# A decoder layer on one core: the sample group's value steps stand one tile later in the cross-attention's output projection

## The chip, the cores and the metric

The kernel runs on one core of a Trainium2 chip. The metric is the device time of one execution in microseconds (us): the median of the timed runs. A profile is one execution of the same program, recorded by the hardware profiler.

## What is computed

One layer of a hybrid decoder for 512 prompt tokens and 64 sample tokens (8 samples of 8 tokens), which share all weights: a mixing block (Mamba-2 heads and mLSTM heads), then cross-attention to a memory, then a SwiGLU block, each with a norm ahead of it and another behind it. The change lies in the cross-attention:

```python
u = _rms(x) * g_pre_x
qx = (u @ w_xq).reshape(bsz, length, X_HEADS, X_HEAD_DIM)
sc = jnp.einsum('blhd,bmhd->bhlm', qx, mem_k) * (X_HEAD_DIM ** -0.5)
pr = jax.nn.softmax(sc, axis=-1)
o = jnp.einsum('bhlm,bmhd->blhd', pr, mem_v).reshape(bsz, length, X_WIDTH) @ w_xo
x = x + _rms(o) * g_post_x
```

There are 4 heads of 256 and 256 memory entries. The prompt's keys and values are computed from its memory; each of the 8 samples has its own cached keys and values, read from HBM. All is in float32.

## The kernel before

Activations lie feature by token: 8 blocks of 128 features, 576 tokens, of which 0 to 511 are the prompt's and 512 to 575 the samples'. A float32 product is made of three matmuls in a faster format: each operand is split into a high part (a copy by ScalarE, ACT, L180 for weights) and a low part (the rest, by VectorE, DVE, L187), and high x high (L202), high x low (L203) and low weight x high (L205) are added up in PSUM (`gemm`, L195).

**The output projection** (L1492 to L1531) has 8 tiles of 128 output features, j = 0 to 7, counted from 0 here. Its first pass takes the tokens 0 to 287 (`EHALVES[0]`); a second pass over the tokens 288 to 575 follows from a written-out plan. A tile has 8 blocks of 3 matmuls with 288 columns. `xo(j, 0)` takes a PSUM bank and asks `split_w` (L172) for the tile's weights: a 512 KB load on SyncE's queue (SP) into one of two buffers `raw`, a cast to `whi` on ACT, a subtraction to `wlo` on DVE. A `raw` buffer is free when the tile two before is split. The split weights of tiles 0 to 3 and 7 come from one pool of three, those of 4, 5 and 6 from another; so tile 3 takes the place of tile 0. The blocks go in the order 2 to 7, then 0 and 1, because the blocks 0 and 1 are head 0's output, which is written last (`attn_values`, the matmuls `ps_ov` of L1372 to L1374, ACT's and DVE's split L191 and L192). Tiles 0 to 2 are given as six blocks and then, in order behind each other, two blocks. Tile 3 does its low-weight products late. After a tile ACT squares it (L264, L268) and scales it (L1504), and DVE adds the squares (L269).

**The samples' attention** is a chain of generators that are advanced a half at a time. `attn_samples_v(hb)` (L1426) does the values for four samples. `pick` (L1389) loads a sample's cached values in two parts of 512 KB (`cached`, L1383, on SP's queue) into a ring of buffers; three are called kva, one kvb. For each part four narrow matmuls (L1399, one a head, weights 128 x 32, 256 columns) go into a bank `ps_os`. Two samples, so 4 loads and 16 matmuls, make a half; the profile counts two records for each of these matmuls, 32 a half. DVE then picks the wanted rows (L1405, L1407). After the second half PE transposes the result (L1432), ACT copies it to the high part of the attention output's sample columns (L1436) and DVE writes the low part (L1437). These columns are read by the second pass only. The last generator, `attn_samples_v(0)`, is not advanced inside the loop over heads; its two halves are left for the projection.

**What sets the order.** The kernel is written with a tile framework whose scheduler orders the instructions of each engine by a timeline model. `with tc.issue_after(m.ins)` holds what is written in the block behind instruction m; `sample_step(m)` (L1270) advances the generator inside such a block. `ends[j]` is the last matmul of tile j. The loads that a step issues belong to it, so they move with it in SP's queue; each waits until the matmuls that read the ring's buffer before are done.

Of the kernel before, what the change touches and what calls it, by code (L numbers as in the profile page):

```python
# [115 lines left out]
def build(nc, tc, ctx, I, O):  # L116
# [593 lines left out]
    for g in range(2):  # L710
# [13 lines left out]
        for h in range(8):  # L724
            k, j = h % 2, (8 * g + h) // 2
# [542 lines left out]
    steps = iter(())  # L1268

    def sample_step(m):  # L1270

        with tc.issue_after(m.ins):
            next(steps, None)
# [137 lines left out]
    def attn_samples_k(hb):  # L1411
        pr, pt = s5[:, 3072 + 256 * hb:3328 + 256 * hb], s5[:, 3584 + 256 * hb:3840 + 256 * hb]
        yield from pick(pr, hb, I["kc"], lambda h, d: qsm[:, 2 * h + d, 32 * hb:32 * hb + 32], "ps_sa")
        mx = at.tile([P, 1], F32, name="mxs")
        sm = at.tile([P, 1], F32, name="sms")
        V.reduce_max(mx, pr, axis=AX.X)
        V.tensor_scalar(mx, mx, -1.0 / 16.0, None, op0=ALU.mult)
        A.activation(pr, pr, AF.Exp, scale=1.0 / 16.0, bias=mx, accum_out=sm)
        V.reciprocal(sm, sm)
        V.tensor_scalar(pr, pr, sm, None, op0=ALU.mult)  # L1420
        pst = (B0, B1)[hb]("ps_pts")
        for m in range(2):
            TE.transpose(pst[:, m * P:(m + 1) * P], pr[:, m * P:(m + 1) * P], ident)
        A.copy(pt, pst[:, 0:256])

    def attn_samples_v(hb):  # L1426
        pt, ot = s5[:, 3584 + 256 * hb:3840 + 256 * hb], s5[:, 4096 + 256 * hb:4352 + 256 * hb]
        tt = slice(TP + 32 * hb, TP + 32 * hb + 32)
        yield from pick(ot, hb, I["vc"], lambda h, m: pt[:, m * P + 32 * h:m * P + 32 * h + 32], "ps_os")
        pst = (B0, B1)[hb]("ps_ots")  # L1430
        for dv in range(2):
            TE.transpose(pst[:, dv * P:(dv + 1) * P], ot[:, dv * P:(dv + 1) * P], ident)  # L1432
        p4 = pst[:, 0:256].rearrange("p (d h t) -> p h d t", d=2, h=4)
        oh4 = oh[:, :, tt].rearrange("p (h d) t -> p h d t", d=2)
        ol4 = ol[:, :, tt].rearrange("p (h d) t -> p h d t", d=2)
        A.copy(oh4, p4)  # L1436
        V.tensor_tensor(ol4, p4, oh4.bitcast(F32), op=ALU.subtract)  # L1437
# [29 lines left out]
    for h in range(3, -1, -1):  # L1467
# [11 lines left out]
        steps = attn_samples_k(h - 2) if h > 1 else attn_samples_v(h)  # L1479
# [12 lines left out]
    def xo(j, i, pool=None):  # L1492

        t0, n = EHALVES[i]

        with tc.issue_after(evx[j - 3].ins if j > 2 else ovs[5].ins):
            ps, w = GP("ps_xo")[:, :n], weights(("xo", j), I["wxo"][j], pool=pool, cut=1024)

        def step(k0, k1):
            m = gemm(ps, [(*w, KT)], act(oh), act(ol), t0, n, k0, k1, [2, 3, 4, 5, 6, 7, 0, 1], 6 if j == 3 else 0)  # L1500
            if k1 < KT:
                return m
            add_sq(ph, ssq, ps, j if i == 0 else XO1.index(j), n, t0=t0)
            evx.append(A.activation(f[:, j, t0:t0 + n], ps, AF.Copy, scale=PAR("g_postx", j)))  # L1504
            return m, evx[-1]
        return step
# [10 lines left out]
    for j in range(8):  # L1517
        step = xo(j, 0, wx if 3 < j < 7 else None)
        if j < 3:

            step(0, KT - 2)
            with tc.issue_after(ends[-1].ins) if j else ExitStack():
                ends.append(step(KT - 2, KT)[0])
        else:
            ends.append(step(0, KT)[0])

        if j == 1:
            next(steps, None)
        elif j == 4:
            sample_step(ends[-1])  # L1530
    kxs.close()  # L1531
    u3l = SL(5, "u3l", F32R)
# [821 lines left out]
```

## Time and profile before

| | us |
|---|---|
| runs | 1088.58, 1088.96, 1090.29 |
| median | 1088.96 |
| profiled execution | 1087.01 |
| its span, first to last instruction | 1085.2 |
| TensorE busy in it | 1075.0 |

The output projection's first pass runs from about 624 us to 660 us of the span. In the profile, PE is TensorE, PEld its weight loads, DVE VectorE, ACT ScalarE, POOL GpSimd, and SPq the issuing of DMAs by SyncE. A row of the timeline gives the start, the us until the last of its instructions ended, the engine, the source line, the operation, output and inputs by the program's names, the shape and the count; in square brackets stands the idle time of that engine ahead of it and what ended it. Matmuls are pipelined, so rows overlap. A row on DMAs gives what was loaded, the queue, the count, the size, and the median us from issue to landing.

### The profile page before, as it was taken

To read this page: it belongs to the slowest core of one execution; us is meant where nothing else is said; L and a number is where in the kernel's file an instruction comes from. 1 tells how busy PE (TensorE), PEld (TensorE's weight loads), DVE (VectorE), ACT (ScalarE), POOL (GpSimd) and SP (SyncE) were. 2 spreads that over 40 slices of the span, in tenths; PEclk is the share of its full clock that TensorE was granted. 3 is DMA by queue.
4 is the path that set the end of the run, shared out by engine and by line. 5 is a ranking of instruction groups with operands and counts; after the bars stand their busy time and mean duration, and the time that the engine had idled before them with its cause. 6 is when DMAs were issued, how large, how long until landed. Compare 5 with 4: busy or idle time off the path is not lost.

```text
span 1085.2 us, 20708 instructions
## 1 busy us (share of the span) xinstructions
PE 1075.0 (99%) x8124; PEld 1022.1 (94%) x8124; DVE 752.4 (69%) x1507; ACT 610.9 (56%) x1098; POOL 228.0 (21%) x305
## 2 busy tenths in 40 slices
PE   9999999999999999999999999999999999999997
PEld 9999887778999999999999989999999999999997
DVE  6896785658877775568755546766467887787556
ACT  7867632355654555656555545645566566656653
POOL 1332643313113111000154301100011111111000
PEclk9999999999999999999999999999999999999999
DMA  6775535435654449653458775643486697578532
GB/s 211 179 159 126 161 111 172 165 80 185 190 152 144 110 123 324 226 193 101 152 194 288 271 252 180 239 133 92 135 176 137 159 203 163 117 189 184 125 131 88
DMA packets 58966, 182.29 MB, mean 168 GB/s; under 512 B 6604, under 2 KB 11852, under 8 KB 58356
## 3 DMA queue, kind: packets, MB, share of 16 engines
q1 hardware_dynamic: 42740, 138.06, 38.6%
q0 software_dynamic: 15552, 41.95, 19.6%
q8 instruction: 64, 1.05, 0.4%
q10 hardware_dynamic: 576, 0.95, 0.3%
q14 instruction: 34, 0.28, 0.1%
HBM read 160.28 MB, written 20.65 MB: 167 GB/s over the span
## 4 chain that ended last, share of the span: by engine, by line
PE 86%; DVE 5%; ACT 4%; issue 2%; DMA 2%; POOL 0%; DVEq 0%; SPq 0%; ACTq 0%; POOLq 0%
PE ps_in L203 4%; PE ps_in L202 4%; PE ps_in L205 4%; PE ps_v L815 3%; PE ps_o L205 3%; PE ps_o L203 3%; PE ps_g L1846 3%; PE ps_g L1847 3%; PE ps_o L202 3%; PE ps_u L1847 3%; PE ps_u L1848 3%; PE ps_u L1846 3%; PE ps_g L1848 3%; PE ps_dn L1846 2%; PE ps_dn L1847 2%
## 5 line engine op out<-in xcount | busy, mean ns | idle before, releaser
L202 PE MATMUL ps_in<-uh,whi 128*128 128x320 f32 (+1 forms) x544 | 162.9, 300 | 0.5 <-DVE cb L451 0.5
L205 PE MATMUL ps_in<-uh,wlo 128*128 128x320 f32 (+1 forms) x544 | 162.3, 299 | 0.3 <-DMA wlo<-win 0.3
L203 PE MATMUL ps_in<-ul,whi 128*128 128x320 f32 (+1 forms) x544 | 161.8, 298 | 0.0
L180 ACT CAST whi<-raw 128x1024 fp32r<-128x1024 f32 (+1 forms) x104 | 105.2, 1013 | 100.0 <-PE ps_in L203 25.9
L187 DVE TENSOR_TENSOR wlo<-raw,whi 128x512 fp32r<-128x512 f32 (+1 forms) x96 | 93.7, 978 | 75.1 <-ACT whi L180 74.0
L202 PEld LDWEIGHTS ps_in<-uh,whi 128*128 128x128 f32 x544 | 102.8, 189 | 3.3 <-issue 1.7
L205 PEld LDWEIGHTS ps_in<-uh,wlo 128*128 128x128 f32 x544 | 102.3, 188 | 1.5 <-DMA wlo<-win 0.5
L203 PEld LDWEIGHTS ps_in<-ul,whi 128*128 128x128 f32 x544 | 102.4, 188 | 0.6
L185 POOL DMA_DIRECT2D wlo<-win x32 | 27.8, 869 | 80.7 <-ACT wlo L184 70.0
L1847 PE MATMUL ps_g<-b,whi 128*128 128x288 f32 x144 | 42.5, 295 | 0.0
L1846 PE MATMUL ps_g<-b,whi 128*128 128x288 f32 x144 | 42.4, 295 | 0.0
L1847 PE MATMUL ps_u<-b,whi 128*128 128x288 f32 x144 | 42.4, 295 | 0.0
L1846 PE MATMUL ps_u<-b,whi 128*128 128x288 f32 x144 | 42.2, 294 | 0.0
L1819 ACT CAST whi<-rawx 128x1024 fp32r<-128x1024 f32 (+1 forms) x26 | 25.6, 984 | 27.9 <-PE ps_dn L1847 13.8
L192 DVE TENSOR_TENSOR wlo<-sw,whi 128x1024 fp32r<-128x1024 f32 (+1 forms) x26 | 29.6, 1140 | 14.9 <-ACT whi L191 14.8
L202 PE MATMUL ps_xo<-qh,whi 128*128 128x288 f32 x128 | 38.5, 303 | 0.2 <-ACT whi L180 0.2
L205 PE MATMUL ps_o<-mixm_h,wlo 128*128 128x256 f32 (+1 forms) x128 | 37.9, 296 | 0.0
L1798 ACT CAST whi<-raw 128x1024 fp32r<-128x1024 f32 (+1 forms) x26 | 25.6, 983 | 21.8 <-PE ps_g L1847 9.7
L203 PE MATMUL ps_xo<-ql,whi 128*128 128x288 f32 x128 | 37.8, 296 | 0.0
L205 PE MATMUL ps_o<-mixs_h,wlo 128*128 128x320 f32 (+1 forms) x128 | 37.7, 295 | 0.0
L203 PE MATMUL ps_o<-mixs_l,whi 128*128 128x320 f32 (+1 forms) x128 | 37.7, 295 | 0.0
L203 PE MATMUL ps_o<-mixm_l,whi 128*128 128x256 f32 (+1 forms) x128 | 37.7, 295 | 0.0
(769 smaller groups left out, 3853.6 us busy)
## 6 DMA issues: line engine op xcount, KB each, us to landing
raw<-win SPq DMA_DIRECT2D x35, 512.0 KB, 4.0
raw<-wout SPq DMA_DIRECT2D x17, 512.0 KB, 3.7
raw<-wxq SPq DMA_DIRECT2D x13, 512.0 KB, 6.0
raw<-wgate SPq DMA_DIRECT2D x13, 512.0 KB, 3.6
raw<-wup SPq DMA_DIRECT2D x13, 512.0 KB, 5.1
wlo<-win POOLq DMA_DIRECT2D x24, 256.0 KB, 5.1
kva<-vc SPq DMA_DIRECT2D x11, 512.0 KB, 5.0
raw<-wv SPq DMA_DIRECT2D x10, 512.0 KB, 4.0
```

The lines of the kernel that those rows point to most:

```text
L180: casts.append(A.copy(hi[:, :n], raw[:, :n]))
L185: G.dma_start(lo[:, a:b], src[:, a:b], accum_op=ALU.add)
L187: e.tensor_tensor(lo[:, a:b], raw[:, a:b], hi[:, a:b].bitcast(F32), op=ALU.subtract)
L192: (eng or V).tensor_tensor(lo, src, hi.bitcast(F32), op=ALU.subtract)
L202: mm(ps, wh, ah, start=i == 0, stop=False)
L203: mm(ps, wh, al, start=False, stop=False)
L205: m = mm(ps, tiles[order[c]][1], xh(order[c], t0, n), start=False, stop=c == len(tiles) - 1)
L815: mm(ps, a, b, skip_group_check=True, **kw)
L1798: s.c1 = A.copy(s.h1[:, s.all], s.r1[:, s.all])
L1846: mm(ps, wh, b[0][k], start=start and k == 0, stop=False, skip_group_check=True)
L1847: mm(ps, wh, b[1][k], start=False, stop=False, skip_group_check=True)
L1848: m = mm(ps, wl, b[0][k], start=False, stop=k == nk - 1, skip_group_check=True)
```

## The change

Before, the first half of the last generator was advanced after tile 1 was written, without `issue_after`, so that the scheduler could place it anywhere that its data allowed; the second half was advanced behind tile 4's last matmul. Now both are advanced by `sample_step`, behind the last matmul of tile 2 and of tile 5. Counted from 0, that is ahead of tiles 3 and 6 in place of 2 and 5.

```diff
         else:
             ends.append(step(0, KT)[0])
 
-        if j == 1:
-            next(steps, None)
-        elif j == 4:
+        if j in (2, 5):
             sample_step(ends[-1])
     kxs.close()
```

The kernel after has two lines fewer from there on, so a line of the profile above L1527 is lower by two in its profile.

## The prediction

> **What bounds the kernel now.** I read the page first: busy time by engine and the chain that ended last.
>
> ```profile
> PE 1075.0 (99%) x8124; PEld 1022.1 (94%) x8124; DVE 752.4 (69%) x1507; ACT 610.9 (56%) x1098; POOL 228.0 (21%) x305
> PE 86%; DVE 5%; ACT 4%; issue 2%; DMA 2%; POOL 0%; DVEq 0%; SPq 0%; ACTq 0%; POOLq 0%
> ```
>
> TensorE (PE) is busy for 1075.0 of 1085.2 us and is 86% of the chain, so what the change adds to or takes from PE's path inside the output projection is found again at the end. No matmul is added or dropped. What can move the time is the price of the order: switches between matmul shapes, and waits. So next I read PE's timeline of the stage, 624 to 664 us. Its columns are start, time until the last of the row ended, engine, line, names, shape and count; what a matmul costs is the distance to the next start, since they overlap.
>
> ```profile
> 629.92 0.30 PE L205 MATMUL ps_xo<-qh,wlo 128*128 128x288 f32 x1
> 630.14 0.64 PE L1399 MATMUL ps_os<-kva 128*32 128x256 f32 x8
> 630.71 0.40 PE L202 MATMUL ps_xo<-qh,whi 128*128 128x288 f32 x1
> 630.95 0.30 PE L203 MATMUL ps_xo<-ql,whi 128*128 128x288 f32 x1
> 631.09 0.29 PE L205 MATMUL ps_xo<-qh,wlo 128*128 128x288 f32 x1
> 631.31 0.62 PE L1399 MATMUL ps_os<-kva 128*32 128x256 f32 x2
> 631.86 0.50 PE L1372 MATMUL ps_ov<-prh,mv 128*128 128x512 f32 x1
> 632.29 0.63 PE L1399 MATMUL ps_os<-kva 128*32 128x256 f32 x6
> 632.86 0.40 PE L202 MATMUL ps_xo<-qh,whi 128*128 128x288 f32 x1
> 633.10 0.30 PE L203 MATMUL ps_xo<-ql,whi 128*128 128x288 f32 x1
> ...
> 635.44 0.39 PE L1373 MATMUL ps_ov<-prl,mv 128*128 128x512 f32 x1
> 635.66 0.39 PE L1374 MATMUL ps_ov<-prh,mv 128*128 128x512 f32 x1
> 635.98 0.64 PE L1399 MATMUL ps_os<-kva 128*32 128x256 f32 x8
> ...
> 636.98 0.40 PE L202 MATMUL ps_xo<-qh,whi 128*128 128x288 f32 x1
> 637.22 0.29 PE L203 MATMUL ps_xo<-ql,whi 128*128 128x288 f32 x1
> ...
> 639.33 0.29 PE L205 MATMUL ps_xo<-qh,wlo 128*128 128x288 f32 x1
> ...
> 640.93 0.29 PE L205 MATMUL ps_xo<-qh,wlo 128*128 128x288 f32 x1
> 641.45 0.40 PE L202 MATMUL ps_xo<-qh,whi 128*128 128x288 f32 x1 [0.22 <-ACT whi L180]
> 641.69 0.30 PE L203 MATMUL ps_xo<-ql,whi 128*128 128x288 f32 x1
> ...
> 647.78 0.29 PE L205 MATMUL ps_xo<-qh,wlo 128*128 128x288 f32 x1
> 648.00 1.50 PE L1399 MATMUL ps_os<-kva 128*32 128x256 f32 x24
> ...
> 649.87 0.40 PE L202 MATMUL ps_xo<-qh,whi 128*128 128x288 f32 x1
> 650.11 0.29 PE L203 MATMUL ps_xo<-ql,whi 128*128 128x288 f32 x1
> ...
> 653.15 0.29 PE L202 MATMUL ps_xo<-qh,whi 128*128 128x288 f32 x1
> ```
>
> The reader is to see: the samples' narrow matmuls (128*32; 32 records a batch, 24 from kva and 8 from kvb) stand in one piece at 648.00 but in pieces between 630.14 and 636.98, and one hole of 0.22 us stands before tile 3 at 641.45. Tiles are counted from 0 throughout, as the loop does: 629.92 ends tile 1's first part, 641.45 opens tile 3, 649.87 tile 5, 653.15 tile 6. A projection matmul costs (653.15 - 650.11) / 23 = 0.132 us, a 512-wide one 635.66 - 635.44 = 0.22 to 0.23.
>
> **The change, part by part.** The scheduler decides, so I compared the order in which the two built programs issue. In the changed one the first batch stands in one piece after tile 2's last matmul, in front of tile 3; the second stands in front of tile 6. All before tile 2 is the same, and all behind the first tile of the second token half, but for a few waits.
>
> 1. *First batch in one piece.* A whole batch lengthens the path from 647.78 to 650.11 by 2.33 - 2 x 0.132 = 2.07. In pieces it costs 630.95 - 629.92 - 0.26 = 0.77; from 631.09 to 633.10 it costs 2.01 less one wide and two projection matmuls (0.49), so 1.52; from 635.66 to 637.22 it costs 1.56 - 0.23 - 0.13 = 1.20. That is 3.49, so one piece saves 1.42 us.
>
> 2. *The hole before tile 3.* From 640.93 to 641.69 go 0.76 us where two matmuls need 0.26. The batch now stands there, and its switch is paid in point 1: another 0.50 saved, if tile 3's weights are cast in time (checked in point 3).
>
> 3. *A new wait in tile 0's tail.* The last six matmuls of tiles 0 and 1 need the last attention head's output, which ACT and DVE write after PE's last ps_ov matmul. Before, that chain lay beside a batch and most of tile 2.
>
> ```profile
> 636.09 0.59 ACT L191 CAST qh<-ps_ov 128x512 fp32r<-128x512 f32 x1 [0.78 <-PE ps_ov L1374]
> 636.71 0.69 DVE L192 TENSOR_TENSOR ql<-ps_ov,qh 128x512 fp32r<-128x512 f32 x1 [0.67 <-ACT qh L191]
> 641.43 1.22 DVE L187 TENSOR_TENSOR wlo<-raw,whi 128x1024 fp32r<-128x1024 f32 x1 [3.12 <-ACT whi L180]
> ```
>
> The low part is ready at 636.71 + 0.69 = 637.40, that is 1.74 after the last ps_ov start (635.66). In the new order the last ps_ov starts at 630.05 + 16 x 0.132 + 11 x 0.23 = 634.69, two matmuls of tile 2 follow, and the fifth of the tail would start at 635.71 but needs the low part of 636.43. With the refill after a wait (the 0.24 instead of 0.13 at 641.45) and 0.05 of response, about 0.88 us is lost. Tile 0 then ends at 636.72, tiles 1 and 2 take 12 x 0.132, the batch starts at 638.52 and tile 3 at 640.39. Before, tile 0's last matmul started at 639.33; tile 3, which waited for the cast behind it, could start 2.12 later (641.45), and its split ended 3.32 later (641.43 + 1.22 = 642.65). Now that is 638.84, in time, and 640.04.
> Parts 1 to 3: -1.42 - 0.50 + 0.88 = -1.04; by the walk 640.39 - 641.45 = -1.06. I take -1.06.
>
> 4. *Tile 5's weights lose their cover.* Here SP's queue matters. SP waits in order. Before, tile 5's load stood behind all four second-half value loads; it now stands behind three (kvb's moves behind it), but each of these waits for a piece of the first batch, and these pieces come later.
>
> ```profile
> 608.84 0.33 SPq L175 DMA_DIRECT2D raw<-wxo  x1
> 609.26 1.08 SPq L1386 DMA_DIRECT2D kva<-vc  x2
> 610.46 0.36 SPq L1386 DMA_DIRECT2D kvb<-vc  x1
> ...
> 636.68 0.33 SPq L1386 DMA_DIRECT2D kva<-vc  x1
> 637.11 1.35 SPq L1386 DMA_DIRECT2D kvb<-vc  x1
> 642.68 0.33 SPq L175 DMA_DIRECT2D raw<-wxo  x1
> ```
>
> ```profile
> kvb<-vc SPq DMA_DIRECT2D x1, 512.0 KB, 6.9
> ```
>
> ```profile
> kva<-vc SPq DMA_DIRECT2D x1, 512.0 KB, 7.2
> ```
>
> ```profile
> kvb<-vc SPq DMA_DIRECT2D x3, 512.0 KB, 6.1
> ```
>
> ```profile
> 646.14 1.05 ACT L180 CAST whi<-raw 128x1024 fp32r<-128x1024 f32 x1 [0.41 <-DMA raw<-wxo]
> 647.28 1.23 DVE L187 TENSOR_TENSOR wlo<-raw,whi 128x1024 fp32r<-128x1024 f32 x1 [1.45 <-ACT whi L180]
> ```
>
> The last number of a kva or kvb row is us from issue to landing. The first of these rows is the load issued at 610.46, the second is the third load of another burst, the third the middle of the stage's three kvb loads. Before, tile 5's load went out at 642.68 with the value loads nearly all landed, landed near 646.1 (3.4 later), was cast and split by 648.51, and first needed at 649.87: the second batch lay in between. Now the third piece of the batch ends at 638.52 + 1.50 = 640.02, its load goes out at 640.08 (SP follows by 0.06), and tile 5's load 0.43 behind it, 640.5; tile 3's split (640.04), which frees its buffer, is no later. Three fresh loads of 512 KB are ahead of it. Tile 5 now follows tile 4 directly: first matmul at 640.39 + 0.11 + 48 x 0.132 = 646.84, the third, which needs the low part, at 647.10. Landing to split takes 2.43, or 2.45 with PE's response. So there is no wait for a landing up to 644.65, 4.15 after issue; beyond that PE loses landing + 2.45 - 647.10, and 0.11 of refill. Bounds for the landing: 3.4 (a lone load) and 7.2. The likest rows are fourth-in-burst loads, 6.9 (behind the three at 608.84 and 609.26) and 6.1; I take 6.5, so 647.0, and a loss of 2.35 + 0.11 = 2.46 us.
>
> The DMA page of the Trainium skill, "DMA: Bandwidth & Descriptors", in "Queues, rings and completion order", says that each DMA engine takes descriptors in ring order; by that the load waits for the three ahead, which the 6.9 against 3.4 bears out. [...]
>
> 5. *What I cost at nothing.* GpSimd's queue is unchanged. DVE's two reads of the first batch move behind tile 3's and 4's splits; only the transposes some 15 us later wait for them. kvb's load moves behind tile 5's: its reader, the second batch, is 10 us off. Tile 6's cast moves behind tile 4's evacuation and tile 7's ahead of tile 5's; tile 6 starts a batch and 24 matmuls after tile 5, so each has over 2 us. The last transposes (L1432) go from tile 6 to the sixth matmul of tile 7, with 18 x 0.132 = 2.4 us of matmuls behind them instead of over 5, and their ACT copy now stands behind a 1.05 us cast. That cast starts when tile 6 is evacuated, about a microsecond before the transposes, so about half a microsecond is to spare; without it the second token half would wait, microsecond for microsecond.
>
> **Sum:** -1.06 + 2.46 = +1.4 us. The profiled execution took 1087.01 us (span 1085.2), 1.95 below the median of the runs shown, 1088.96; on the median that is 1090.4.
>
> **Rivals.**
> - *The load lands as if alone.* 3.4 us after issue, 643.9, no wait at tile 5; parts 1 to 3 stay: -1.06, so 1087.9. For it: the load at 642.68 did that. Against: three value loads go out within 1.3 us ahead of it.
> - *Slower, by sharing.* If the loads in flight share the engines' time, tile 5's lands with the last of five (kvb behind it too). Four loads took from 608.84 to 610.46 + 6.9 = 617.36, so 8.5 us; beyond a lone 3.4 that is 1.7 each. From the first issue, 638.52 + 0.64 + 0.06 = 639.2, five land by 639.2 + 3.4 + 4 x 1.7 = 649.4, PE loses 4.86, net +3.8, so 1092.8. It ends slower by over 0.2% from a landing 7.3 after issue. For it: the 7.2 of a third-in-burst load. Against: the 6.1.
> - *The change does nothing*: the scheduler could have put the batches back. The issue order rules that out.
>
> **How the numbers follow.** 0.2% is about what a measurement of this kernel can tell from no change: 2.2 us here. My forecast, a wait of 1.5 to 3.3 us at tile 5 with a net between +0.4 and +2.2, gets 0.60; the lone landing, and landings up to +0.4, 0.19, of which 0.03 for over 2.2 us gained by something unseen; sharing, or a wait that I cost at nothing, 0.21. So faster 0.03, within 0.76, slower 0.21. The range runs from the first rival less half a microsecond, 1087.4, to the 7.2 us landing (+2.1) and some way into the sharing case, 1091.8.
>
> **What would show it.** Right: one batch before tile 3 with no hole; a wait on ACT or DVE for ql in tile 0's tail; tile 3 about 1 us earlier; then tile 5 waiting 2 to 3 us for whi or wlo, and the cast in front waiting for raw<-wxo; tile 6 about 1.4 us later than 653.15. Wrong: tile 5 without a wait (the landing was misjudged), tile 3 not earlier (parts 1 to 3), or a wait at the second token half (part 5).

## The result and the profile after

| | us |
|---|---|
| before, beside the changed kernel | 1088.77 (1087.69 to 1090.29) |
| after | 1093.10 (1092.04 to 1093.38) |
| ratio | 1.0038, 95% interval 1.0025 to 1.0051 |
| profiled execution of after, its span | 1092.55, 1090.8 |

So the change costs 4.3 us; 1.4 were forecast, and the time lies outside the range. The page of the changed kernel looks as the old one did:

```profile
PE 1078.0 (99%) x8124; PEld 1025.2 (94%) x8124; DVE 753.5 (69%) x1507; ACT 611.5 (56%) x1098; POOL 227.4 (21%) x305
```

As many matmuls as before, 3.0 us more of busy TensorE, in a span 5.6 us longer. An unchanged count with more busy time means that some matmuls became dearer, which the page alone can't place. PE's timeline of the stage, with the columns as before, does:

```profile
630.41 0.30 PE L205 MATMUL ps_xo<-qh,wlo 128*128 128x288 f32 x1
...
636.46 0.29 PE L202 MATMUL ps_xo<-qh,whi 128*128 128x288 f32 x1
636.99 0.40 PE L203 MATMUL ps_xo<-ql,whi 128*128 128x288 f32 x1 [0.23 <-DVE ql L192]
637.22 0.29 PE L205 MATMUL ps_xo<-qh,wlo 128*128 128x288 f32 x1
...
638.81 0.29 PE L205 MATMUL ps_xo<-qh,wlo 128*128 128x288 f32 x1
639.04 1.50 PE L1399 MATMUL ps_os<-kva 128*32 128x256 f32 x24
...
640.90 0.40 PE L202 MATMUL ps_xo<-qh,whi 128*128 128x288 f32 x1
...
647.22 0.29 PE L205 MATMUL ps_xo<-qh,wlo 128*128 128x288 f32 x1
649.68 0.40 PE L202 MATMUL ps_xo<-qh,whi 128*128 128x288 f32 x1 [2.16 <-ACT whi L180]
649.91 0.29 PE L203 MATMUL ps_xo<-ql,whi 128*128 128x288 f32 x1
650.99 0.61 PE L205 MATMUL ps_xo<-qh,wlo 128*128 128x288 f32 x1 [0.79 <-DVE wlo L187]
651.40 0.44 PE L202 MATMUL ps_xo<-qh,whi 128*128 128x288 f32 x1
651.64 0.44 PE L203 MATMUL ps_xo<-ql,whi 128*128 128x288 f32 x1
...
656.20 0.44 PE L205 MATMUL ps_xo<-qh,wlo 128*128 128x288 f32 x1
656.57 1.68 PE L1399 MATMUL ps_os<-kva 128*32 128x256 f32 x24
...
658.61 0.40 PE L202 MATMUL ps_xo<-qh,whi 128*128 128x288 f32 x1
```

The row at 630.41 was at 629.92 before: this execution reaches the stage 0.49 us later, and that much is taken off below. The reader is to see four things. The first batch now stands in one piece before tile 3 (639.04). Tile 3 follows it at 640.90 without a hole. Tile 5 waits twice, 2.16 us for its cast and 0.79 for its low part. And from 651.40 to 656.20 the matmuls start 0.24 us apart, not 0.132, and a record lasts 0.44, not 0.29, although nothing waits any more. Tile 6 comes at 658.61 - 0.49 = 658.12, against 653.15 before: 4.97 later.

The load behind that wait, in the issues of SP's queue, in the two loads of the stage's weights by themselves (the last number is us from issue to landing; the first row is tile 5's, the second tile 6's), and in the cast that waited for it:

```profile
639.74 1.28 SPq L1386 DMA_DIRECT2D kva<-vc  x3
641.11 0.56 SPq L175 DMA_DIRECT2D raw<-wxo  x1
```

```profile
raw<-wxo SPq DMA_DIRECT2D x1, 512.0 KB, 7.4
```

```profile
raw<-wxo SPq DMA_DIRECT2D x1, 512.0 KB, 8.8
```

```profile
648.58 1.04 ACT L180 CAST whi<-raw 128x1024 fp32r<-128x1024 f32 x1 [3.40 <-DMA raw<-wxo]
```

Tile 5's weights go out right behind three value loads, as forecast, and land 7.4 us later. The slow matmuls are explained by the windows of the same stretch: PE, PEld, DVE, ACT and POOL busy with their counts, then the granted clock of TensorE, the DMA share and GB/s.

```profile
647.50:649.50 2.00, 0.02 (x1) 0.00 (x0) 0.00 (x0) 0.92 (x1) 0.00 (x0) 1.00 1.01 414
649.50:650.50 1.00, 0.53 (x2) 0.30 (x2) 0.79 (x1) 0.83 (x3) 0.00 (x0) 0.83 0.44 180
650.50:651.50 1.00, 0.51 (x2) 0.51 (x3) 0.81 (x2) 0.38 (x1) 0.00 (x0) 0.50 0.01 4
653.00:655.00 2.00, 2.00 (x11) 2.00 (x9) 0.42 (x1) 0.34 (x1) 0.00 (x0) 0.50 0.71 217
656.50:658.00 1.50, 1.50 (x25) 0.80 (x28) 0.93 (x2) 0.80 (x2) 0.00 (x0) 0.84 0.09 14
658.00:660.00 2.00, 2.00 (x26) 1.51 (x15) 0.97 (x2) 0.00 (x0) 0.00 (x0) 1.00 0.83 238
```

The granted clock falls to 0.50 during these waits and stays there, with TensorE fully busy, until about 657.0. Its edges come from the mixed windows: 0.83 over one microsecond leaves 0.34 at half clock, so it fell at about 650.2, when the first standing was over and the second began; 0.84 over 1.5 leaves 0.48, so it rose at about 657.0. That is 6.8 us at half clock. From the third matmul of tile 5 (650.99) to tile 6 (658.61) pass 7.62 us. At full clock the same work takes 0.24 + 20 x 0.132 + 0.22 + 1.87 = 4.97. **The clock costs 2.65 us, more than half of what tile 6 is late.**

### The profile page after: what moved, and what is told of

It is laid out like the page before. It is cut to its first block, busy times and chain, and to the rows that moved or that the text cites. A ratio compares the mean times of both kernels' runs of the same rounds, so it can differ in the third digit from the quotient of the medians.

```text
span 1090.8 us, 20709 instructions
## 1 busy us (share of the span) xinstructions
PE 1078.0 (99%) x8124; PEld 1025.2 (94%) x8124; DVE 753.5 (69%) x1507; ACT 611.5 (56%) x1098; POOL 227.4 (21%) x305
## 4 chain that ended last, share of the span: by engine, by line
PE 88%; DVE 5%; DMA 3%; ACT 2%; issue 2%; POOL 0%; SPq 0%; DVEq 0%; ACTq 0%; POOLq 0%
PE ps_in L203 5%; PE ps_in L202 5%; PE ps_in L205 5%; PE ps_v L815 3%; PE ps_o L205 3%; PE ps_o L203 3%; PE ps_g L1844 3%; PE ps_g L1845 3%; PE ps_u L1845 3%; PE ps_o L202 3%; PE ps_u L1846 3%; PE ps_g L1846 3%; PE ps_u L1844 3%; PE ps_dn L1844 2%; PE ps_dn L1845 2%; PE ps_dn L202 2%
## 5 line engine op out<-in xcount | busy, mean ns | idle before, releaser
L180 ACT CAST whi<-raw 128x1024 fp32r<-128x1024 f32 (+1 forms) x104 | 105.3, 1014 | 100.8 <-PE ps_in L203 25.5
L205 PE MATMUL ps_xo<-qh,wlo 128*128 128x288 f32 x128 | 38.4, 306 | 0.8 <-DVE wlo L187 0.8
```

The lines of the kernel that those rows point to most:

```text
L180: casts.append(A.copy(hi[:, :n], raw[:, :n]))
L205: m = mm(ps, tiles[order[c]][1], xh(order[c], t0, n), start=False, stop=c == len(tiles) - 1)
```

## The experiments

The theory after this reading: (a) the first half's move puts three value loads ahead of tile 5's weights; (b) the second half's move takes away the batch that lay over their way; (c) TensorE then stands long enough for its clock to be halved, and that is paid on top of the wait. The rivals: the later tiles or the new order of batches are dear by themselves; or the half clock has to do with the transfers in flight or the particular work, and not with the standing.

**w5_early.** The changed kernel, with tile 5's weights loaded before any value load of this stage, into space that is free by then.

```diff
+        if j == 2:
+            raw5 = f[:, 6:8, :].rearrange("p a t -> p (a t)")[:, 0:1024]
+            S.dma_start(raw5, I["wxo"][5])
```

`split_w` leaves out its own load for j = 5 and reads `raw5`.

> The changed kernel, with tile 5's weights loaded ahead of the projection's loads into a free part of the output tile, so that no value load is ahead of them. Theory (late weights, then a slow TensorE clock behind the wait): no wait at tile 5, its matmuls 0.13 us apart, granted clock 1.00 there, tile 3 still 1.0 us earlier than in the kernel before; about 1087.7, 1.0 under the kernel before and 5.3 under the changed one. Rival (the batches' new places or the burst of value loads slow the matmuls by themselves): no wait, but matmuls of tile 5 still about 0.24 us apart, so 1090 to 1091.

Measured: 1087.21 us (1086.55 to 1089.39) beside 1088.04 of before, ratio 0.9994 (0.9985 to 1.0002). PE's waits from 600 to 670 us (what waited for what, us, times, longest), and the second batch in its timeline:

```profile
PE ps_xo L204 <- DVE ql L193: 0.2, 1, 0.2
```

```profile
650.56 0.29 PE L206 MATMUL ps_xo<-qh,wlo 128*128 128x288 f32 x1
650.78 1.50 PE L1400 MATMUL ps_os<-kva 128*32 128x256 f32 x24
...
652.64 0.40 PE L203 MATMUL ps_xo<-qh,whi 128*128 128x288 f32 x1
```

(Its lines are one or two higher, for the added ones.) The list of waits has one row: no wait at tile 5. The second batch follows tile 5's last matmul without a gap and costs what it did before (652.64 - 650.56 - 0.13 = 1.95, 1.96 in front of tile 5 before), and the loss is gone. What is left of the change is the gain of parts 1 to 3, 0.83 us by the medians where 1.06 was worked out. Its median is the lowest of all the kernels here, but its interval reaches 1.0002, so that it beats the kernel before is not shown. The late places of the batches are not dear by themselves.

**fill26.** The changed kernel with 26 projection matmuls, whose result nobody reads, between tile 4 and tile 5, so that TensorE waits as long for the weights but does not stand.

```diff
+        elif j == 5:
+            fill = MP("ps_fill")[:, :288]
+            with tc.issue_after(ends[-1].ins):
+                for _ in range(26):
+                    m = mm(fill, weights(("xo", 4), None)[0][:, 0:P], oh[:, 2, 0:288], start=True, stop=True)
+            with tc.issue_after(m.ins):
+                ends.append(step(0, KT)[0])
```

> The changed kernel, with 26 matmuls of 128x288 between tiles 4 and 5 whose result is not used: 3.4 us of work in the place of the wait. Theory (the idle time lets the clock drop): PE is never idle for over about 0.5 us there, clock 1.00, tile 5's matmuls 0.13 us apart; about 2.5 us under the changed kernel, 1090.6, although it does more. Rival (the slow matmuls come from the traffic of the loads or from the order): tile 5 still at 0.24 us, time of the changed kernel, 1093.

Measured: 1090.98 us (1090.49 to 1091.37), ratio to before 1.0028 (1.0017 to 1.0039). So it does 26 matmuls more and is 2.1 us shorter than the changed kernel. PE's timeline:

```profile
647.14 3.60 PE L1528 MATMUL ps_fill<-qh,whi 128*128 128x288 f32 x26
650.57 0.30 PE L202 MATMUL ps_xo<-qh,whi 128*128 128x288 f32 x1
...
651.20 0.40 PE L205 MATMUL ps_xo<-qh,wlo 128*128 128x288 f32 x1 [0.20 <-DVE wlo L187]
651.43 0.29 PE L202 MATMUL ps_xo<-qh,whi 128*128 128x288 f32 x1
...
654.31 1.50 PE L1399 MATMUL ps_os<-kva 128*32 128x256 f32 x24
```

Tile 5's third matmul comes about when it did in the changed kernel (651.20 against 650.99), with the same load as late. But from there to the second batch it takes 3.11 us, 5.58 in the changed one. The granted clock stays at 1.00 (the number behind POOL's in the window of the whole stage):

```profile
640.00:660.00 20.00, 19.80 (x175) 17.98 (x168) 8.84 (x14) 7.11 (x14) 0.00 (x0) 1.00 0.69 236
```

The wait is still paid, the clock is not: this separates the two, and with the same loads in flight it is the standing that halves the clock in this stage.

**wait1, wait2, wait3.** The other way round: the kernel before, where no load is late, with one, two or three ACT copies of tile 5's high weights onto themselves, which change nothing in them, behind tile 4. Tile 6 is held behind tile 5, so that nothing else fills the wait.

```diff
+        elif j == 5:
+            hi = weights(("xo", 5), None)[0]
+            with tc.issue_after(evx[4].ins):
+                for _ in range(1):
+                    A.copy(hi, hi.bitcast(F32))
+            ends.append(step(0, KT)[0])
+        elif j == 6:
+            with tc.issue_after(ends[-1].ins):
+                ends.append(step(0, KT)[0])
```

> The kernel before, with one more 1.05 us copy of tile 5's high weights onto themselves behind tile 4's evacuation, so that PE waits about 1.7 us ahead of tile 5 for ACT, with no load involved. Theory: the clock drops if 1.7 us is enough; then the matmuls behind run at 0.24 us for some 6 us and the time is 1.7 + 2.5 over the kernel before, 1093; if 1.7 us is too short, 1090.5. Rival (no clock effect, the slow stretch belongs to the loads): 1090.5 with 0.13 us.

> As the run with one more copy, with two: PE waits about 2.6 us ahead of tile 5, broken by two small transposes. Theory: granted clock 0.5 behind it for some 6 us, 2.6 + 2.5 over the kernel before, 1094. Rival (no clock effect): 2.6 over it, 1091.4, matmuls 0.13 us apart.

> As the runs with one and two more copies in the kernel before, with three: PE waits 3.5 to 4.5 us ahead of tile 5, for ACT alone, broken by two small transposes. Theory (idle time alone lowers the clock, if it is long enough): granted clock 0.5 behind the wait and 0.24 us a matmul for some 5 us or more; about 4 + 2.5 over the kernel before, 1094.5. Rival (the clock drop belongs to the loads): 4 over it, 1092, matmuls 0.13 us apart.

Measured, ratio to the kernel before beside each:

| | us | ratio (95%) |
|---|---|---|
| wait1 | 1089.59 (1088.43 to 1091.42) | 1.0014 (1.0004 to 1.0023) |
| wait2 | 1091.48 (1089.88 to 1092.72) | 1.0033 (1.0022 to 1.0043) |
| wait3 | 1094.15 (1093.53 to 1095.22) | 1.0057 (1.0044 to 1.0071) |

With one copy PE stands 1.40 us and goes on at 0.13 us a matmul, in PE's timeline of wait1:

```profile
652.18 0.40 PE L202 MATMUL ps_xo<-qh,whi 128*128 128x288 f32 x1 [1.40 <-ACT whi L1528]
652.42 0.29 PE L203 MATMUL ps_xo<-ql,whi 128*128 128x288 f32 x1
652.55 0.29 PE L205 MATMUL ps_xo<-qh,wlo 128*128 128x288 f32 x1
```

With three it stands 2.06 and 1.68 us, two short transposes between, and goes on at 0.24, in PE's timeline of wait3:

```profile
653.52 0.41 PE L1432 MATMUL ps_ots<-c,kva 128*128 128x128 f32 x2 [2.06 <-DVE kva L1407]
655.61 0.46 PE L202 MATMUL ps_xo<-qh,whi 128*128 128x288 f32 x1 [1.68 <-ACT whi L1528]
655.87 0.44 PE L203 MATMUL ps_xo<-ql,whi 128*128 128x288 f32 x1
656.11 0.44 PE L205 MATMUL ps_xo<-qh,wlo 128*128 128x288 f32 x1
```

Its windows:

```profile
655.00:656.00 1.00, 0.39 (x2) 0.39 (x3) 1.00 (x2) 0.83 (x2) 0.00 (x0) 0.90 0.09 33
656.00:657.00 1.00, 1.00 (x6) 1.00 (x5) 0.29 (x1) 0.00 (x0) 0.00 (x0) 0.50 0.38 33
658.00:660.00 2.00, 2.00 (x12) 2.00 (x12) 0.00 (x0) 0.00 (x0) 0.00 (x0) 0.69 0.46 182
```

No load is late there, and the matmuls come at half clock all the same, by the edges (0.90 over 1 us, 0.69 over 2) from 655.8 to 659.24, 3.4 us. So the transfers and the change's own order are not needed for it. The median of wait2 is what the rival gave for it (1091.4, against 1094 by the theory). Its executions spread over 2.8 us, and its profiled one, the shortest, stood 2.56 us and kept its clock. That left open whether the rest of the spread is the clock, so the same kernel was profiled three times more, on another chip.

> The same kernel as the one with two copies, looked at once more. Theory: idle of TensorE of about 2.6 us lies at the edge, so an execution of 1090.5 us or more shows matmuls 0.24 us apart for some stretch behind the wait, one of about 1090 shows none. Rival: the longer executions are longer for another reason, so at 1091 or more the matmuls behind the wait are still 0.13 us apart.

> As the look before: slow matmuls behind the wait in an execution of 1090.5 us or more, none in one of about 1090; by the rival none in either.

> As the two looks before: slow matmuls behind the wait in an execution of 1090.5 us or more, none in one of about 1090; by the rival none in any.

These executions took 1093.14, 1093.34 and 1091.28 us, beside one of 1088.81 of the kernel before on that chip. All three show the half clock behind waits of 2.34, 2.46 and 2.28 us, each shorter than the one that did without. The last of them (wait2_d) is set against wait2's, which came into the stage at nearly the same time; PE's timeline and windows of wait2_d, then of wait2:

```profile
652.59 0.41 PE L1432 MATMUL ps_ots<-c,kva 128*128 128x128 f32 x2 [2.28 <-DVE kva L1407]
...
653.81 0.44 PE L203 MATMUL ps_xo<-ql,whi 128*128 128x288 f32 x1
```

```profile
652.60:653.70 1.10, 1.10 (x9) 1.10 (x10) 0.11 (x1) 1.10 (x3) 0.00 (x0) 1.00 0.76 302
653.70:657.00 3.30, 3.30 (x16) 3.30 (x15) 1.46 (x2) 0.14 (x1) 0.00 (x0) 0.50 0.43 107
657.00:659.00 2.00, 2.00 (x16) 2.00 (x16) 0.46 (x1) 0.80 (x2) 0.00 (x0) 0.97 0.39 160
```

```profile
652.80 0.41 PE L1432 MATMUL ps_ots<-c,kva 128*128 128x128 f32 x2 [2.56 <-DVE kva L1407]
```

```profile
654.00:657.00 3.00, 3.00 (x25) 3.00 (x24) 1.49 (x3) 0.61 (x3) 0.00 (x0) 1.00 0.42 123
```

In wait2_d the clock falls only after TensorE has worked again for a microsecond, at 653.7, and it is back at about 657.1 (0.97 over 2 us): 3.4 us. In wait2 it stays at 1.00 over the same stretch. The 16 matmuls that wait2_d starts in 3.30 us need 16 x 0.132 = 2.1 at full clock, so the half clock costs it about 1.2 us; the whole times are not set against each other, since the chips differ. The other two were some 2 us late before the wait (their transposes start at 654.54 and 654.75), and that part of their length has another cause. So the length of one wait does not decide alone: at this length one execution falls and another does not, and the last section says what differed.

**first_only, second_only and the changed kernel again (after_again).** One half of the change each: `if j in (2, 4)` with `sample_step`, and the first half as before with the second at `j == 5`.

> The first half of the samples' step behind tile 2 as in the changed kernel, the second behind tile 4 as before. Theory (tile 5's weights are late because the first half moved, and the wait is bare because the second moved): the batch lies in tile 5's wait again, what is left of it is 1 to 2 us and broken, the clock stays at 1.00; net -1.0 + 1.5, about 1088.5. Rival (the first half's place alone costs it): about 1093.

> The first half wherever its data allows, as before; the second half behind tile 5, as in the changed kernel. Theory: tile 5's load goes out at 642.7 as before, its low part is ready near 648.5 and needed near 648.1, so PE waits about 0.4 us, no clock effect; about 1088.5. Rival (the second half's place alone costs it): about 1093.

> The changed kernel once more, beside the runs below. If the slow stretch behind tile 5's wait hung on where the wait falls in time, some executions would be without it, about 2.5 us shorter (1090.5); if the wait of 2.2 and 0.8 us is always enough, all lie near 1093 and the profile shows tile 5 at 0.24 us a matmul again.

Measured beside 1087.93 of before:

| | us | ratio (95%) |
|---|---|---|
| first half alone | 1088.86 (1087.67 to 1089.48) | 1.0007 (0.9998 to 1.0016) |
| second half alone | 1088.79 (1088.16 to 1090.65) | 1.0010 (1.0002 to 1.0019) |
| both, the changed kernel | 1093.02 (1092.70 to 1093.50) | 1.0046 (1.0032 to 1.0060) |

after_again answers its own question: all five executions lie within 0.8 us, none near 1090.5, and its clock is at 0.50 again, from about 650.7 to 657.5 us (0.69 over 650.5 to 651, 0.98 over 657.5 to 658). With the first result that makes eleven of eleven executions of the changed kernel between 1092.04 and 1093.50. The longest row of PE's waits between 600 and 670 us, for first_only, for second_only, and two rows for after_again:

```profile
PE ps_xo L202 <- ACT whi L180: 0.9, 1, 0.9
```

```profile
PE ps_xo L205 <- DVE wlo L187: 0.5, 1, 0.5
```

```profile
PE ps_xo L202 <- ACT whi L180: 2.3, 1, 2.3
PE ps_xo L205 <- DVE wlo L187: 0.5, 1, 0.5
```

With the first half alone the load is as late (issued at 642.46, its cast starts at 650.13, 7.7 later), but the second batch stands in the wait and takes most of it. With the second half alone the batch is gone, but the load goes out with no burst ahead of it (issued at 644.72, cast at 648.46, 3.7 later). The clock stays at 1.00 from 640 to 660 us in both. Each costs about 0.9 us by the medians, together 1.8, though the interval of the first half alone reaches 0.9998, so that it costs anything is not shown; both at once cost 5.1. The change's price lies in the two meeting: only together do they make a wait long enough to cost the clock as well.

## Where the prediction was right and where wrong

- **Parts 1 and 2, the batch in one piece and the hole: right.** From tile 2's last matmul (638.81) to tile 3 (640.90) pass 2.09 us; 640.39 - 638.52 + 0.22 is the same.
- **Part 3, the wait in tile 0's tail: right.** It is there for ql, between 636.46 and 636.99, with a shorter one ahead of it: from tile 0's first matmul of these six (635.69) to the sixth (637.22) pass 1.53 us where five need 0.66, so 0.87 is lost where 0.88 was worked out. The whole walk gave tile 3 at 640.39; measured 640.90 - 0.49 = 640.41, so -1.04 for the three parts where -1.06 was taken.
- **Part 4, the lost cover: the mechanism right, the size too small.** The load landed 7.4 us after issue. I took 6.5, and 7.2 was my upper bound. It also went out 0.1 later, at 641.11 - 0.49 = 640.62. Wait and refill came to 3.4 + 0.1 = 3.5 us (650.99 against 647.61, where the third matmul would have stood), where I wrote 2.46. With this alone the net would have been -1.04 + 3.5 = +2.4, about 1091.4: just past the +2.2 that the forecast gave as its upper net, and still inside the range.
- **The step that failed is the sum itself:** after part 4 it priced every matmul behind the wait at 0.132 us. The wait brought a term that I had not: 2.65 us of half clock behind it. -1.04 + 3.5 + 2.65 = +5.1; tile 6 measured +4.97. fill26 and wait3 show the term from both sides, without the standing and without the late load; why the clock halved at just that length of wait is in part open (last section).
- **Part 5: held.** From tile 6 to the end of the span only 5.6 - 0.49 - 4.97 = 0.14 us more is lost. Tile 6's load landed late too, 8.8 us, and PE did not wait for it.
- **The rivals.** The lone landing is out. The sharing rival gave 1092.8, close to 1093.1, but not by its own road. It wanted tile 5's load 8.9 us after issue; 7.4 is past the 7.3 from which it would end slower by over 0.2%, yet the wait falls 1.4 us short of its 4.86. The rest of the time came from the clock. That the number is near is chance.

## What to carry to other kernels

A wait of TensorE may cost more than its length: behind one of 2.2 us with 0.8 more after it, the next 7 us ran at half clock and cost another 2.65. So price a gap of some 2 us or more at its length and, beside it, a stretch at the half-clock matmul (0.24 here for 0.132), and look at the granted clock in the windows behind each long wait. When a step is moved, look at its loads twice: at what they now stand ahead of in the queue, and at whether the step itself was the work that covered somebody else's load; two moves that cost 0.9 us each by their medians cost 5.1 together.

## What the runs showed of the hardware

The half clock began while TensorE stood or after it had gone on, and came in pieces of about one length: 3.4 us in wait2_d and in wait3, 6.8 in the changed kernel, which is two of them. A wait of 1.40 us did not bring it in the profiled execution of wait1. In the changed kernel the first standing, 2.16 us, had brought it before the second began; waits of 2.28, 2.34 and 2.46 brought it too, and one of 2.56 did not.

The Trainium skill, "TensorE: Matmul & The Clock Gate", in "🔬 Part 1: The HAM clock gate (the "warmup" mystery)", says that TensorE goes to half rate after an idle window of about 3.4 us and back after a busy one, and that the window runs freely of the program. The lengths here agree, and so do the edges, worked out as above from windows in which the clock is mixed. In the changed kernel the clock falls at 80.1 us (0.53 over 80 to 82), at 650.2 and, with the matmuls done, at 1087.0 (0.76 over 1086 to 1088): 167 and 128 times 3.413 us apart. Counted back in this step from the last fall of wait2 (1084.8; 0.69 over 1084 to 1086), an edge lies at 651.3, inside its wait from 650.24 to 652.80, and cuts the 2.56 us into 1.0 and 1.5. In wait2_d one edge is its fall at 653.7 and the one ahead of it 650.3, and all of its 2.28 us lies between them. So by these edges the place of the wait decided: the longer one was cut by an edge, the shorter was not. The 1.40 us of wait1 was cut too (at 651.9, by its last fall at 1082.0), so it tells little.

Where the trace differs is the fall: no window here was idle throughout. In this stage 2.16 us of standing in one window was enough and 1.5 was not; where between them it turns stays open. Nor is standing all that counts. Ahead of the changed kernel's fall at 80.1 us, TensorE had stood for 0.41 us in 3.4, and the kernel before keeps its clock at 1.00 there; what brought that one stays open. It is no part of what the stage lost: the execution was 0.71 us late before it (a matmul at 77.80 that was at 77.09) and 0.49 after it.
